# Batched transposed matmul on one core: b loaded with four consecutive rows in each partition, the column order restored in the PSUM copy, and stores three batches behind

## The chip, the cores and the metric

The kernel runs on one core of a Trainium2 chip. The metric is the device time of the whole program in microseconds, as a median of several executions. The span of the profile is some 1.6 to 2 us shorter than that time, because it runs from the first instruction to the last. All comparisons below are of runs that were classed as fast, except the two single-look probes, whose state is unknown; of those I use only durations within one trace.

Engine names in the profile: PE is the matmul engine, PEld its weight loads, DVE the vector engine, ACT the scalar engine, SPq the queue of the engine that issues all DMAs. SBUF is the on-chip memory that the DMAs of this kernel load and store, PSUM the one that PE writes its results to; the tiles that this kernel keeps in either have 128 rows (128x512 in the profile), called partitions.

## The reference

```
batch, m, k, n = 16, 512, 512, 512
a: (batch, k, m) float32,  b: (batch, n, k) float32
out = matmul(a transposed to (batch, m, k), b transposed to (batch, k, n))   # float32
```

Each batch reads 1 MiB of a and 1 MiB of b and writes 1 MiB. The total is 50.3 MB of traffic.

## The kernel before

b has n in its rows, and the matmuls of this kernel take k in the partitions. So PE transposes b in 128x128 blocks into PSUM, a copy on DVE casts the result to bf16 in SBUF, and 16 matmuls per batch use it. ACT casts a. The output is copied from PSUM by ACT and DVE in turns, and it is stored six batches later.

```python
a_v = a.rearrange("b (ki ko) m -> b ki ko m", ko=KO)      # 4 consecutive rows per partition: 8 KB
b_v = b.rearrange("b (no ni) k -> b ni no k", ni=P)       # 4 rows, 128 apart: 4 x 2 KB
# a_pool 3, b_pool 3, ac_pool 4, bt_pool 3, o_pool 8 buffers; PSUM: 4 for the transposes, 4 for the output
LAG = 6
for i in range(B):
    # load b, load a, four ACT casts of a (a_bf)                                        [cut]
    for rk in range(KO):
        bt_ps = psum_t.tile([P, N], f32)
        for no in range(NO):
            nc.tensor.transpose(bt_ps[:, no * P:(no + 1) * P], b_sr[:, no, rk, :], identity)
        nc.vector.tensor_copy(bt_sb[:, rk, :], bt_ps)             # fp32 PSUM -> bf16 SBUF
    for rm in range(MO):
        o_ps = psum_o.tile([P, N], f32)
        for rk in range(KO):
            nc.tensor.matmul(o_ps, a_br[:, rk, rm, :], bt_sb[:, rk, :], ...)
        # copy o_ps to o_sb on ACT (rm even) or DVE (rm odd)                              [cut]
    if i >= LAG: emit_out_dma(i - LAG)
```

Of the kernel before, what the change touches and what calls it, by code (L numbers as in the profile page):

```python
# [1 line left out]

# [5 lines left out]


@with_exitstack
def kernel(
    ctx: ExitStack,
    tc: tile.TileContext,
    a: bass.AP,
    b: bass.AP,
    out: bass.AP,
):
    nc = tc.nc
    P = 128  # L20
    B, K, M = a.shape
    _, N, _ = b.shape
    KO = K // P
    MO = M // P
    NO = N // P

    f32 = mybir.dt.float32
    cdt = mybir.dt.bfloat16

    a_v = a.rearrange("b (ki ko) m -> b ki ko m", ko=KO)  # L30
    b_v = b.rearrange("b (no ni) k -> b ni no k", ni=P)
    out_v = out.rearrange("b (mi mo) n -> b mi mo n", mo=MO)

    const = ctx.enter_context(tc.tile_pool(name="const", bufs=1))
    identity = const.tile([P, P], f32)
    make_identity(nc, identity)

    a_pool = ctx.enter_context(tc.tile_pool(name="a_pool", bufs=3))
    b_pool = ctx.enter_context(tc.tile_pool(name="b_pool", bufs=3))
    ac_pool = ctx.enter_context(tc.tile_pool(name="ac_pool", bufs=4))  # L40
    bt_pool = ctx.enter_context(tc.tile_pool(name="bt_pool", bufs=3))
    o_pool = ctx.enter_context(tc.tile_pool(name="o_pool", bufs=8))
    psum_t = ctx.enter_context(tc.tile_pool(name="psum_t", bufs=4, space=bass.MemoryType.PSUM))
    psum_o = ctx.enter_context(tc.tile_pool(name="psum_o", bufs=4, space=bass.MemoryType.PSUM))

    LAG = 6
    o_tiles = {}

    def emit_out_dma(j):
        nc.sync.dma_start(out_v[j], o_tiles.pop(j))  # L50

    for i in range(B):
        b_sb = b_pool.tile([P, NO, K], f32)
        nc.sync.dma_start(b_sb, b_v[i])
        a_sb = a_pool.tile([P, KO, M], f32)
        nc.sync.dma_start(a_sb, a_v[i])  # L56

        a_bf = ac_pool.tile([P, KO, M], cdt)
        for rk in range(KO):
            nc.scalar.copy(a_bf[:, rk, :], a_sb[:, rk, :])  # L60
        a_br = a_bf.rearrange("p rk (pm rm) -> p rk rm pm", rm=MO)

        b_sr = b_sb.rearrange("p no (pk rk) -> p no rk pk", rk=KO)
        bt_sb = bt_pool.tile([P, KO, N], cdt)
        for rk in range(KO):
            bt_ps = psum_t.tile([P, N], f32)
            for no in range(NO):
                nc.tensor.transpose(  # L68
                    bt_ps[:, no * P:(no + 1) * P],
                    b_sr[:, no, rk, :],  # L70
                    identity,
                )
            nc.vector.tensor_copy(bt_sb[:, rk, :], bt_ps)  # L73

        o_sb = o_pool.tile([P, MO, N], f32)
        o_tiles[i] = o_sb
# [3 lines that stand above are left out]
                nc.tensor.matmul(  # L80
                    o_ps,
                    a_br[:, rk, rm, :],
                    bt_sb[:, rk, :],
                    start=(rk == 0),
                    stop=(rk == KO - 1),
                )
            if rm % 2 == 0:
                nc.scalar.copy(o_sb[:, rm, :], o_ps)  # L88
            else:
                nc.vector.tensor_copy(o_sb[:, rm, :], o_ps)  # L90

        if i >= LAG:
            emit_out_dma(i - LAG)

    for j in range(B - LAG, B):
        emit_out_dma(j)


# [1 line left out]
_INS = ['a', 'b']  # L100
_OUTS = [((16, 512, 512), 'float32')]


# [23 lines left out]
```

## Time and profile before

| | before |
|---|---|
| time | 129.39 us (129.38 to 129.58) |
| span of the profile | 127.8 us |
| DMA, mean rate over the span | 394 GB/s |
| PE / DVE / ACT busy | 72% / 48% / 43% |
| DVE cast of bt_sb | 683 ns |

These lines of the page show the busy share by engine, the busy tenths in 40 equal slices of the span for PE, DVE and DMA, what the DMA moved in each slice, and the packets.

```profile
PE 92.5 (72%) x504; PEld 60.6 (47%) x512; DVE 61.5 (48%) x96; ACT 54.8 (43%) x97; POOL 0.7 (1%) x6
...
PE   0099999999999995768767796877779777670000
...
DVE  0053668586774865463544727355472635640000
...
DMA  3999999999999999999999999999999999999980
GB/s 90 402 370 422 406 399 420 382 409 398 404 417 415 417 419 394 416 410 429 420 410 423 406 436 405 416 426 413 427 402 431 412 424 418 426 428 428 426 346 36
DMA packets 13063, 50.42 MB, mean 394 GB/s; under 512 B 768, under 2 KB 768, under 8 KB 8960
```

The DMA row is the one without gaps: the kernel is bound by DMA. PE is full only from the 3rd slice to the 15th (to 48 us), where it works through batches whose loads came faster than it could follow.

The group of lines for the cast of b gives its duration (busy us, mean ns of one, then idle time before it and who ended it):

```profile
L73 DVE CAST bt_sb<-bt_ps 128x512 bf16<-128x512 f32 x64 | 40.0, 683 | 14.7 <-PE bt_ps L68 14.7
```

### The profile page before, as it was taken

The numbers are of one execution on the slowest core, as the hardware profiler recorded it, in microseconds if no ns is written. First come the engines' busy times: TensorE is split into PE (matmuls) and PEld (weight loads), VectorE is DVE, ScalarE is ACT, GpSimd is POOL, SyncE is SP. The second block draws the span as 40 slices with busy tenths as digits, with TensorE's granted clock in tenths as the row PEclk, the third lists the DMA queues.
The fourth block names the chain that finished last, engine by engine and source line by source line (L and its number), as shares of the span: only waits on it lengthen the run. The fifth ranks groups of instructions, "written<-read, shape, count | busy, mean of one in ns | idle before, by whom it ended". The sixth has DMA issues, their size and how long they took to land.

```text
span 127.8 us, 1405 instructions
## 1 busy us (share of the span) xinstructions
PE 92.5 (72%) x504; PEld 60.6 (47%) x512; DVE 61.5 (48%) x96; ACT 54.8 (43%) x97; POOL 0.7 (1%) x6
## 2 busy tenths in 40 slices
PE   0099999999999995768767796877779777670000
PEld 0094858678586763364634536353364634430000
DVE  0053668586774865463544727355472635640000
ACT  4026747646674635407163460816337072540000
POOL 2000000000000000000000000000000000000000
PEclk9999999999999999999999999999999999998555
DMA  3999999999999999999999999999999999999980
GB/s 90 402 370 422 406 399 420 382 409 398 404 417 415 417 419 394 416 410 429 420 410 423 406 436 405 416 426 413 427 402 431 412 424 418 426 428 428 426 346 36
DMA packets 13063, 50.42 MB, mean 394 GB/s; under 512 B 768, under 2 KB 768, under 8 KB 8960
## 3 DMA queue, kind: packets, MB, share of 16 engines
q1 hardware_dynamic: 13056, 50.33, 97.5%
q8 instruction: 4, 0.07, 0.2%
q14 instruction: 3, 0.02, 0.0%
HBM read 33.55 MB, written 16.78 MB: 394 GB/s over the span
## 4 chain that ended last, share of the span: by engine, by line
DMA 50%; PE 34%; SPq 3%; ACT 1%; issue 1%; DVE 1%; ACTq 0%
DMA a_sb<-in_a_dram 32%; PE o_ps L80 22%; DMA out_dram<-o_sb 13%; PE bt_ps L68 12%; DMA b_sb<-in_b_dram 4%; SPq L56 3%; ACT a_bf L60 1%; DVE o_sb L90 1%; ACT o_sb L88 0%; ACTq L60 0%; SPq L50 0%
## 5 line engine op out<-in xcount | busy, mean ns | idle before, releaser
L80 PE MATMUL o_ps<-bt_sb,a_bf 128*128 128x512 bf16 x248 | 59.0, 385 | 9.1 <-ACT a_bf L60 8.7
L60 ACT CAST a_bf<-a_sb 128x512 bf16<-128x512 f32 x64 | 34.9, 615 | 39.6 <-DMA a_sb<-in_a_dram 39.5
L73 DVE CAST bt_sb<-bt_ps 128x512 bf16<-128x512 f32 x64 | 40.0, 683 | 14.7 <-PE bt_ps L68 14.7
L68 PE MATMUL bt_ps<-identity,b_sb 128*128 128x128 f32 x256 | 35.7, 295 | 12.8 <-DMA b_sb<-in_b_dram 12.8
L80 PEld LDWEIGHTS <-a_bf 128*128 128x128 bf16 x256 | 27.3, 115 | 35.8 <-ACT a_bf L60 17.7
L68 PEld LDWEIGHTS bt_ps<-identity,b_sb 128*128 128x128 f32 x256 | 33.9, 211 | 17.5 <-PE o_ps L80 8.5
L90 DVE COPY o_sb<-o_ps 128x512 f32<-128x512 f32 x32 | 22.1, 692 | 38.9 <-PE o_ps L80 21.9
L88 ACT COPY o_sb<-o_ps 128x512 f32<-128x512 f32 x32 | 18.8, 586 | 19.0 <-PE o_ps L80 18.9
L60 ACT ACT_TABLE_LOAD x1 | 1.3, 1283 | 0.7 <-PEq L111 0.7
masks.py:199 POOL TENSOR_SCALAR_AFFINE_SELECT identity<-identity 128x128 f32<-128x128 f32 x1 | 0.3, 292 | 0.1
masks.py:197 POOL MEMSET identity<- 128x128 f32 x1 | 0.2, 204 | 0.3 <-POOLq L111 0.3
L111 POOL MEMSET const-bfloat16-1.0<- 128x1 bf16 x1 | 0.1, 101 | 0.0
L111 POOL MEMSET const-uint8-127<- 128x1 uint8 x1 | 0.1, 101 | 0.0
L111 POOL MEMSET const-float32-0.0<- 128x1 f32 x1 | 0.1, 98 | 0.2 <-issue 0.2
L111 POOL MEMSET const-float32-1.0<- 128x1 f32 x1 | 0.1, 98 | 0.0
## 6 DMA issues: line engine op xcount, KB each, us to landing
b_sb<-in_b_dram SPq DMA_DIRECT2D x16, 1024.0 KB, 15.4
a_sb<-in_a_dram SPq DMA_DIRECT2D x16, 1024.0 KB, 17.3
out_dram<-o_sb SPq DMA_DIRECT2D x16, 1024.0 KB, 17.4
```

Of the source, the lines that this page charges most:

```text
L56: nc.sync.dma_start(a_sb, a_v[i])
L60: nc.scalar.copy(a_bf[:, rk, :], a_sb[:, rk, :])
L68: nc.tensor.transpose(bt_ps[:, no * P:(no + 1) * P], b_sr[:, no, rk, :], identity,)
L73: nc.vector.tensor_copy(bt_sb[:, rk, :], bt_ps)
L80: nc.tensor.matmul(o_ps, a_br[:, rk, rm, :], bt_sb[:, rk, :], start=(rk == 0), stop=(rk == KO - 1),)
L88: nc.scalar.copy(o_sb[:, rm, :], o_ps)
L90: nc.vector.tensor_copy(o_sb[:, rm, :], o_ps)
L111: nc = _bacc.Bacc("TRN2", target_bir_lowering=False, num_devices=1)
```

## The change

The intent is to make the loads of b cheaper. With rows 4p to 4p+3 in partition p, each partition gets one contiguous piece of 8 KB instead of four of 2 KB. The transposed blocks then hold every fourth column, so the copy from PSUM puts the columns back in order by writing bf16 with a step of four elements, 8 bytes. Along with that the stores come three batches behind, and the buffers are redistributed.

```diff
-    b_v = b.rearrange("b (no ni) k -> b ni no k", ni=P)
+    b_v = b.rearrange("b (ni no) k -> b ni no k", no=NO)
...  a_pool 3 -> 5, b_pool 3 -> 5, ac_pool 4 -> 3, o_pool 8 -> 6 buffers
-    LAG = 6
+    LAG = 3
...
+        bt_w = bt_sb.rearrange("p rk (ni no) -> p rk no ni", no=NO)
         for rk in range(KO):
-            bt_ps = psum_t.tile([P, N], f32)
+            bt_ps = psum_t.tile([P, NO, P], f32)
...          transposes: same blocks
-            nc.vector.tensor_copy(bt_sb[:, rk, :], bt_ps)
+            nc.vector.tensor_copy(bt_w[:, rk, :, :], bt_ps)
```

More of the change, by code (lines that the diff above doesn't have):

```diff
@@ L36 @@
     make_identity(nc, identity)
-    a_pool = ctx.enter_context(tc.tile_pool(name="a_pool", bufs=3))
-    b_pool = ctx.enter_context(tc.tile_pool(name="b_pool", bufs=3))
-    ac_pool = ctx.enter_context(tc.tile_pool(name="ac_pool", bufs=4))
+    a_pool = ctx.enter_context(tc.tile_pool(name="a_pool", bufs=5))
+    b_pool = ctx.enter_context(tc.tile_pool(name="b_pool", bufs=5))
+    ac_pool = ctx.enter_context(tc.tile_pool(name="ac_pool", bufs=3))
     bt_pool = ctx.enter_context(tc.tile_pool(name="bt_pool", bufs=3))
-    o_pool = ctx.enter_context(tc.tile_pool(name="o_pool", bufs=8))
+    o_pool = ctx.enter_context(tc.tile_pool(name="o_pool", bufs=6))
     psum_t = ctx.enter_context(tc.tile_pool(name="psum_t", bufs=4, space=bass.MemoryType.PSUM))
     psum_o = ctx.enter_context(tc.tile_pool(name="psum_o", bufs=4, space=bass.MemoryType.PSUM))
-    LAG = 6
+    LAG = 3
     o_tiles = {}
-    def emit_out_dma(j):
-        nc.sync.dma_start(out_v[j], o_tiles.pop(j))
     for i in range(B):
@@ L64 @@
         bt_sb = bt_pool.tile([P, KO, N], cdt)
+        bt_w = bt_sb.rearrange("p rk (ni no) -> p rk no ni", no=NO)
         for rk in range(KO):
-            bt_ps = psum_t.tile([P, N], f32)
+            bt_ps = psum_t.tile([P, NO, P], f32)
             for no in range(NO):
-                nc.tensor.transpose(
-                    bt_ps[:, no * P:(no + 1) * P],
-                    b_sr[:, no, rk, :],
-                    identity,
-                )
-            nc.vector.tensor_copy(bt_sb[:, rk, :], bt_ps)
+                nc.tensor.transpose(bt_ps[:, no, :], b_sr[:, no, rk, :], identity)
+            nc.vector.tensor_copy(bt_w[:, rk, :, :], bt_ps)
         o_sb = o_pool.tile([P, MO, N], f32)
@@ L92 @@
         if i >= LAG:
-            emit_out_dma(i - LAG)
+            nc.sync.dma_start(out_v[i - LAG], o_tiles.pop(i - LAG))
     for j in range(B - LAG, B):
-        emit_out_dma(j)
+        nc.sync.dma_start(out_v[j], o_tiles.pop(j))
 _INS = ['a', 'b']
```

## The prediction

> **What bounds the kernel.** The 16 DMA engines. The page's slices show DMA at 9 (90% or more) in 37 of 40, 97.5% of the span on one queue; PE is busy 72%, DVE 48%, ACT 43%. The chain that ended last is half DMA; its PE half is the first 44 us, where the table of windows shows the DMA just as busy (400 to 410 GB/s). Packets run from 1.9 us to about 1.2 us before the span's end (127.8 us; the measured time is 1.6 us more). So only cheaper DMA traffic, or a gap in it, moves the time; the bytes (50.3 MB) stay.
>
> **The traffic.** b arrives as 8192 packets of 2 KB, a and out as 4096 of 8 KB. With four consecutive rows per partition b becomes 2048 packets of 8 KB. In the trace's packet records a 2 KB packet takes 84 ns (mean 86), an 8 KB one 309 (mean 313): 4 x 86 - 313 = 32 ns saved, x 2048 / 16 engines = 4.1 us. But successive packets overlap, small ones more: fitting the length of busy windows to the packets in them gives 82.5 and 310 ns, 2.5 us. Window rates agree: 403 GB/s where only a and b load, 417 with all three, 429 for stores alone, so b runs at 390 to 398 against about 425, 2.6 to 3.3 us over 16 MiB. [...] this trace shows several per cent at 2 KB, small but on the bounding resource. I take 3 us, all on the critical path.
>
> **The PSUM copy** now writes bf16 with a step of 8 bytes (683 ns now). [...] DVE has slack: 6 x 0.69 = 4.1 us of work per batch of about 7.2 us. PE and ACT: unchanged.
>
> **Lag 3, five load buffers.** Stores mix with loads earlier. No starvation: a store waits for the compute of three batches ago while 6 MB or more (over 14 us) are queued. The tail: after the last a lands, four stores remain (now seven), 2.45 us each on an engine, so the last store must be queued within 7.4 us of that landing. Landing to last copy took 5.1 us (110.0 to 115.1), plus 0.4 before it and 1.1 from issue to first packet: 6.7 us. It just fits on the slowest engine; faster engines may idle without setting the end. So lag costs 0 to 0.7 us and gains nothing.
>
> **Prediction.** 129.4 - 3.0 = 126.4 us, 8 in 10 within 125.3 to 127.6. Faster by over 2%: 0.60; within 2%: 0.38; slower: 0.02.
>
> **What would show it right or wrong.** DMA view: about 6,900 packets in all, mean rate from 394 to about 404 GB/s, DMA still 9 nearly throughout; b's packets at about 312 ns; the cast of bt_sb below 0.75 us; the last store issued before those ahead of it end, with perhaps a short dip of DMA just before the end.
>
> **What would make it wrong.** 8 KB loads mixed with stores running slower than now; a slow strided copy (over 1.2 us), which would delay the last batch and open a gap in the tail; small packets costing only what the fit of the later half says (80.4 and 309.8 ns, about 1.5 us)[...].

The sum of the forecast is 129.4 - 3.0 = 126.4 us, where the 3.0 us come from the packet records and window rates. The PSUM copy had no term in it. It was put at 0.75 us at most, and as that was below what DVE had to spare, it entered the sum with nothing. That bound was not worked out from a trace.

## More of the kernel before

How long does compute take for a batch when nothing holds it up? The timeline of the kernel before, in that first part, shows it (columns: start us, duration us, engine, line, operation, operands, count).

```profile
19.52 2.07 PE L68 MATMUL bt_ps<-identity,b_sb 128*128 128x128 f32 x16
...
20.33 2.48 DVE L73 CAST bt_sb<-bt_ps 128x512 bf16<-128x512 f32 x4
...
21.43 3.62 PE L80 MATMUL o_ps<-bt_sb,a_bf 128*128 128x512 bf16 x16
...
24.89 2.08 PE L68 MATMUL bt_ps<-identity,b_sb 128*128 128x128 f32 x16
```

From one group of transposes to the next is 24.89 - 19.52 = 5.37 us.

## The result

The changed kernel takes 134.68 us (134.66 to 134.71, 4 runs) against 129.40 us for the kernel before on the same chip. The ratio is 1.041 with a 95% interval of 1.040 to 1.043: slower by 4%. Here and below a ratio is the mean time of one kernel's fast runs over that of the other's fast runs of the same rounds, so it is not quite the ratio of the medians quoted beside it. The output is correct.

The same lines of the page, after:

```profile
PE 97.1 (73%) x504; PEld 62.4 (47%) x512; DVE 96.9 (73%) x96; ACT 53.3 (40%) x97; POOL 0.7 (1%) x6
...
PE   0297959786886959687786959788695959788620
...
DVE  0096787969597786959696896959687795959720
...
DMA  3999999999999999999999999999999999925124
GB/s 118 424 419 427 434 427 318 429 392 422 419 429 432 429 424 429 419 424 429 429 424 427 422 424 429 427 419 429 424 424 432 427 429 424 404 106 237 79 118 200
DMA packets 6919, 50.42 MB, mean 379 GB/s; under 512 B 768, under 2 KB 768, under 8 KB 768
```

Two things stand out. In mid-run (slices 11 to 34) the DMA moves 426 GB/s on average, where the kernel before moved 416, so the larger packets do what they should. But from the 36th slice on the DMA row falls from 9 to 2, 5, 1, 2, 4: for the last 16 us the DMA engines mostly wait. Busy time of DVE went from 61.5 to 96.9 us, and one group accounts for it:

```profile
L71 DVE CAST bt_sb<-bt_ps 128x512 bf16<-128x512 f32 x64 | 76.0, 1327 | 6.8 <-PE bt_ps L70 6.8
```

The copy with a step takes 1327 ns instead of 683. The timeline shows what that does to one batch:

```profile
21.35 2.08 PE L70 MATMUL bt_ps<-identity,b_sb 128*128 128x128 f32 x16
...
22.16 4.76 DVE L71 CAST bt_sb<-bt_ps 128x512 bf16<-128x512 f32 x4
...
23.54 0.59 PE L78 MATMUL o_ps<-bt_sb,a_bf 128*128 128x512 bf16 x2
...
26.97 1.89 PE L78 MATMUL o_ps<-bt_sb,a_bf 128*128 128x512 bf16 x8 [0.34 <-DVE bt_sb L71]
...
28.70 2.09 PE L70 MATMUL bt_ps<-identity,b_sb 128*128 128x128 f32 x16
```

PE transposes; the four copies take 4.76 us instead of 2.48; the last matmuls wait for the fourth copy ("<-DVE bt_sb L71"); and in the order in which PE runs them here the transposes of the next batch come only after those matmuls. The period is now 28.70 - 21.35 = 7.35 us, and 7.55 us from the fourth batch to the last. That is 2.0 to 2.2 us more than before, the 2.28 us that the four copies grew by, nearly.

What does the DMA need per batch? Three transfers at 2.45 us each on an engine (the spacing of completions in the trace's packet records), so 7.4 us. The two periods are nearly equal, and that is why the loss is easily misread. While a batch is in flight the DMA has work, and its row is full. But compute, at 7.5 us per batch from the first batch on, needs 5.7 us (first b landed) + 16 x 7.5 = 126 us before the last output can be stored; it ends at 127.7 us, and the last store lands at 131.7 us, near the end of the span at 132.9 us. In the kernel before, compute could run at 5.4 us per batch while the first loads, without stores between them, were coming in at 403 GB/s (16 to 28 us), an estimated 5.2 us for the two of a batch (2.1 MB); it followed the loads closely and was done at 115.1 us, 5.1 us after the last a was seen to land.

### The profile page after: what moved, and what is told of

Its sections match the earlier page's. It is cut to its first block, busy times and chain, and to the rows that moved or that the text cites. A ratio compares the mean times of both kernels' runs of the same rounds, so it can differ in the third digit from the quotient of the medians.

```text
span 132.9 us, 1387 instructions
## 1 busy us (share of the span) xinstructions
PE 97.1 (73%) x504; PEld 62.4 (47%) x512; DVE 96.9 (73%) x96; ACT 53.3 (40%) x97; POOL 0.7 (1%) x6
## 5 line engine op out<-in xcount | busy, mean ns | idle before, releaser
L78 PE MATMUL o_ps<-bt_sb,a_bf 128*128 128x512 bf16 x248 | 64.8, 378 | 24.2 <-DVE bt_sb L71 22.3
L71 DVE CAST bt_sb<-bt_ps 128x512 bf16<-128x512 f32 x64 | 76.0, 1327 | 6.8 <-PE bt_ps L70 6.8
L78 PEld LDWEIGHTS <-a_bf 128*128 128x128 bf16 x256 | 29.2, 114 | 56.7 <-issue 38.1
L70 PE MATMUL bt_ps<-identity,b_sb 128*128 128x128 f32 x256 | 34.9, 292 | 5.7 <-DMA b_sb<-in_b_dram 5.7
L70 PEld LDWEIGHTS bt_ps<-identity,b_sb 128*128 128x128 f32 x256 | 34.6, 210 | 7.5 <-issue 5.6
```

The lines of the kernel that those rows point to most:

```text
L70: nc.tensor.transpose(bt_ps[:, no, :], b_sr[:, no, rk, :], identity)
L71: nc.vector.tensor_copy(bt_w[:, rk, :, :], bt_ps)
```

## Experiments

The theory (A): the copy with the step of 8 bytes takes twice as long, it stands in a serial chain from PE to DVE and back to PE, and that chain became the limit. The rivals (B): three batches of lag starve the DMA queue, or the 8 KB rows load worse. The wait table of the issuing queue makes the first rival look strong, so it had to be tested. In the changed kernel (columns: us in total, times, longest us):

```profile
SPq L91 <- DVE o_sb L88: 80.4, 13, 10.0
SPq L94 <- DVE o_sb L88: 21.5, 3, 7.2
```

The queue waits 80 us for the compute of three batches ago, which looks like starvation.

### 1. The copy without its step (wrong column order on purpose)

```diff
-            nc.vector.tensor_copy(bt_w[:, rk, :, :], bt_ps)
+            nc.vector.tensor_copy(bt_sb[:, rk, :].rearrange("p (no ni) -> p no ni", no=NO), bt_ps)
```

> The changed kernel, with the PSUM copy writing without a step (so the columns of the output come in the wrong order: wrong on purpose). Theory A (the copy with a step takes twice as long and makes the chain PE, DVE, PE longer than the DMA's time per batch): casts back at 0.68 us, 126 to 127 us, ratio to before 0.975 to 0.985, DMA without the hole at the end. Theory B (three batches of lag starve the DMA queue, or 8 KB rows load more slowly): still 132 us or more.

Measured: 126.58 us (126.39 to 126.72), ratio 0.978 (0.976 to 0.980); casts 683 ns. Everything else of the change is in this kernel, lag included. So the step of the copy is the whole of the loss, and it hides a gain of 2.2%.

### 2. The step alone, in the kernel before (wrong column order on purpose)

```diff
+        bt_w = bt_sb.rearrange("p rk (ni no) -> p rk no ni", no=NO)
-            nc.vector.tensor_copy(bt_sb[:, rk, :], bt_ps)
+            nc.vector.tensor_copy(bt_w[:, rk, :, :], bt_ps.rearrange("p (no ni) -> p no ni", no=NO))
```

> The kernel before, with only the copy's step of four elements added (lag 6, three load buffers, 2 KB rows; columns in the wrong order on purpose). Theory A: 16 batches at 7.5 us after the first b has landed at 6.4 us, plus 5 us of last store: 131 to 135 us, ratio 1.02 to 1.045. Theory B: 129 to 130 us, as before.

Measured: 134.94 us, ratio 1.042 (1.040 to 1.044). The step alone costs as much as the whole change. Once the chain is the limit, cheaper loads are worth little: this kernel with 2 KB rows and the changed one with 8 KB rows are both at 1.04. The kernel that differs from this one by the 8 KB rows alone is that of experiment 3, at 134.24 us. The 0.7 us between them is what the first b gains: the transposes start at 6.33 us here and at 5.69 us there, and the last output copy ends 0.66 us later here.

### 3. The changed kernel with the old lag and buffers

```diff
-    LAG = 3          a 5, b 5, cast a 3, out 6 buffers
+    LAG = 6          a 3, b 3, cast a 4, out 8 buffers
```

> The changed kernel with the old lag of 6 and the old numbers of buffers (a and b 3, cast a 4, out 8). Theory A: the chain of compute is unchanged, 133 to 136 us, ratio 1.03 to 1.05. Theory B: under 128 us, because the DMA queue no longer waits for the compute of three batches ago.

Measured: 134.24 us, ratio 1.037 (1.035 to 1.039). The lag is not the cause: the last output copy ends at 127.7 us in both traces. The 0.4 us by which the time is below that of the changed kernel come after that copy, and what they are was not looked into. The queue's wait did not vanish but moved to another line:

```profile
SPq L53 <- PE bt_ps L70: 75.5, 13, 6.5
SPq L94 <- DVE o_sb L88: 25.2, 4, 7.2
```

Now the loads of b wait 75.5 us for a buffer, which the transposes release. Whatever paces the batches, the issuing queue waits for it somewhere; such a wait tells that the queue is ahead, not that it is starved. In experiment 1 the same wait on L91 was still 40.3 us, at a DMA that was never idle in mid-run.

### 4. The changed kernel's lag and buffers alone, in the kernel before

```diff
-    LAG = 6          a 3, b 3, cast a 4, out 8 buffers
+    LAG = 3          a 5, b 5, cast a 3, out 6 buffers
```

> The kernel before with only the lag of 3 and the new numbers of buffers (2 KB rows, copy without a step). The prediction said that the lag gains nothing and costs 0 to 0.7 us: 129.2 to 130.2 us, ratio 0.998 to 1.006. A rival: the earlier mixing of stores and loads gains by itself, under 128.5.

Measured: 129.53 us against 129.35, ratio 1.0005 (0.999 to 1.002). In this kernel the lag neither gains nor costs.

### 5. A probe of the step

In one kernel, the four copies of each batch write bf16 with steps of 1, 2, 4 and 8 elements, and the matmuls read them back with the same step. Its output is wrong, which doesn't matter for the time. To make room, a and b have 3 buffers here and bt_sb 2.

```diff
+  bt_v = [bt_sb[:, r, :N << r].rearrange("p (n s) -> p s n", s=1 << r)[:, 0, :] for r in range(KO)]
+  if rk == 0:   nc.vector.tensor_copy(bt_v[0], ...)     # L72, step 2 bytes
+  elif rk == 1: nc.vector.tensor_copy(bt_v[1], ...)     # L74, 4 bytes
+  elif rk == 2: nc.vector.tensor_copy(bt_v[2], ...)     # L76, 8 bytes
+  else:         nc.vector.tensor_copy(bt_v[3], ...)     # L78, 16 bytes
+  # matmuls that read bt_v[0..3]: L87, L89, L91, L93
```

> A probe, wrong on purpose: within each batch the four copies from PSUM write bf16 with steps of 1, 2, 4 and 8 elements (2, 4, 8, 16 bytes), each on its own line, and the matmuls read them back with the same step, each on its own line. A1 [...]: 0.68 us at step 1, 1.33 at 2, 4 and 8. A2 (the distance counts): step 2 under 1.0, step 8 well over 1.33. The matmuls that read with a step: 0.38 us for all if reading with a step is free, over 0.5 if not.

Its groups of lines (mean ns is the second number after the bar):

```profile
L93 PE MATMUL o_ps<-bt_sb,a_bf 128*128 128x512 bf16 x64 | 66.2, 1077 | 16.3 <-DVE bt_sb L78 16.3
...
L78 DVE CAST bt_sb<-bt_ps 128x512 bf16<-128x512 f32 x16 | 39.6, 2477 | 0.0
L91 PE MATMUL o_ps<-bt_sb,a_bf 128*128 128x512 bf16 x64 | 37.2, 624 | 1.2 <-DVE bt_sb L76 1.2
...
L89 PE MATMUL o_ps<-bt_sb,a_bf 128*128 128x512 bf16 x64 | 26.4, 450 | 0.1
L87 PE MATMUL o_ps<-bt_sb,a_bf 128*128 128x512 bf16 x56 | 22.8, 447 | 0.4
...
L76 DVE CAST bt_sb<-bt_ps 128x512 bf16<-128x512 f32 x16 | 20.7, 1295 | 0.7
...
L72 DVE CAST bt_sb<-bt_ps 128x512 bf16<-128x512 f32 x16 | 11.0, 688 | 8.5 <-PE bt_ps L70 8.5
L74 DVE CAST bt_sb<-bt_ps 128x512 bf16<-128x512 f32 x16 | 11.8, 739 | 1.3 <-PE bt_ps L70 1.3
```

The DVE write takes 688, 739, 1295 and 2477 ns at steps of 2, 4, 8 and 16 bytes. So hypothesis A1 of the expectation (any step loses) is refuted and A2 (the distance counts) holds: a step of two elements is almost free, and beyond that each doubling of the step about doubles the time. Matmuls that read bt_sb with a step take 447, 450, 624 and 1077 ns by the same lines. These means blur the effect: PE's granted clock was only 0.81 of full speed in this probe, and the profile models where a matmul ends. Two matmuls of the same line in a row start 216 ns apart without a step (at the full clock), 229, 433 and 881 ns apart with steps of 4, 8 and 16 bytes, so reading doubles at the same distances as writing. With 16 matmuls per batch, the step of 8 bytes would have added an estimated 16 x (433 - 216) = 3.5 us per batch to PE, more than the copies lost, so reading bt_sb with a step in the matmul would have been no way out either.

### 6. Two rows in each partition: 4 KB packets and a step of 4 bytes

```diff
-    b_v = b.rearrange("b (ni no) k -> b ni no k", no=NO)
+    b_v = b.rearrange("b (nb ni n2) k -> b ni nb n2 k", ni=P, n2=2)
-        bt_w = bt_sb.rearrange("p rk (ni no) -> p rk no ni", no=NO)
+        bt_w = bt_sb.rearrange("p rk (nb ni n2) -> p rk nb n2 ni", ni=P, n2=2)
```

> The changed kernel with two consecutive rows of b in each partition instead of four: packets of 4 KB, and the copy writes bf16 with a step of 2 elements (4 bytes), which the step probe showed nearly free (0.74 us, 0.63 us apart). Correct result. If the step of the write is the whole cause (A): casts at 0.74 us, 5.5 to 5.7 us per batch where compute is alone, so DMA-bound: 126.6 to 127.8 us, ratio 0.977 to 0.987 (two thirds of the gain of 8 KB packets). If an interleaved write as such were the cause: 131 us or more.

Measured: 126.78 us, ratio 0.981 (0.979 to 0.983), casts 727 ns, correct. An interleaved write is not slow as such; its distance is what counts. The trace's packet records give a median of 159 ns for a 4 KB packet, so 318 ns for 8 KB, against 4 x 84 = 336 ns in packets of 2 KB and 309 ns in one of 8 KB.

### 7. Four ways to restore the order, in one kernel

```diff
+  rk == 1: the transposes write PSUM with a step of 16 bytes (L71), the copy has no step (L77)
+  rk == 0: nc.vector.tensor_copy(bt_sb[:, rk, :] as (ni no), bt_ps.rearrange("p no ni -> p ni no"))   # L75
+  rk == 2: nc.scalar.copy(bt_w[:, rk, :, :], bt_ps)                                                 # L79
+  rk == 3: nc.vector.tensor_copy(bt_w[:, rk, :, :], bt_ps)             # L81, as in the changed kernel
```

> A probe with a correct result: the changed kernel, with the reorder done in four ways, one for each rk of a batch: DVE reads PSUM with a step of 512 bytes and writes without a step; PE writes the transpose into PSUM with a step of 16 bytes and DVE copies without one; ACT copies with the step of 8 bytes; DVE as in the changed kernel (control, 1.33 us). If only writing to SBUF with a step is slow: the first two casts 0.68 us, the transposes as before (about 0.29 us, 0.13 apart). If stepping through PSUM costs as well: over 1.0 us for the first. ACT: 0.6 us if it has no such cost, over 1.0 if it does.

```profile
L73 PE MATMUL bt_ps<-identity,b_sb 128*128 128x128 f32 x192 | 30.0, 294 | 7.0 <-DMA b_sb<-in_b_dram 6.4
...
L81 DVE CAST bt_sb<-bt_ps 128x512 bf16<-128x512 f32 x16 | 20.8, 1298 | 1.9 <-PE bt_ps L73 0.9
L79 ACT CAST bt_sb<-bt_ps 128x512 bf16<-128x512 f32 x16 | 20.7, 1294 | 26.0 <-PE bt_ps L73 26.0
...
L75 DVE CAST bt_sb<-bt_ps 128x512 bf16<-128x512 f32 x16 | 11.0, 687 | 8.8 <-PE bt_ps L73 8.8
L77 DVE CAST bt_sb<-bt_ps 128x512 bf16<-128x512 f32 x16 | 10.9, 682 | 0.2 <-PE bt_ps L71 0.2
L71 PE MATMUL bt_ps<-identity,b_sb 128*128 128x128 f32 x64 | 10.8, 292 | 0.0
```

The result is correct. Reading PSUM with a step of 512 bytes costs nothing (687 ns), and neither does writing the transposes into PSUM with a step of 16 bytes (292 ns against 294, transposes starting 121 ns apart in both, and a copy of 682 ns); no run wrote the 128x512 outputs of the bf16 matmuls with a step. Writing SBUF with the step of 8 bytes costs ACT the same as DVE, 1294 ns, where ACT's copies of the fp32 outputs from PSUM, which write without a step, took 586 ns. The cost belongs to the SBUF side.

### 8. The slow copies kept, but out of the chain

If the loss comes from the chain, then putting the transposes and copies of batch i+1 ahead of the matmuls of batch i should remove it, with the copies as slow as ever. The order on PE and DVE was pinned in the program, so that the scheduler could not restore the old one.

```diff
+    for i in range(B + 1):
+        # loads, casts, transposes and stepped copies of batch i   (if i < B)
+        # matmuls and output copies of batch i - 1                 (if i > 0)
```

> The changed kernel, slow copies and all, but the transposes and copies of batch i+1 are put ahead of the matmuls of batch i on PE and DVE, so the slow copies no longer stand in a serial chain with PE. Correct result. If the loss comes from the serial chain (2.1 transposes to 4.75 copies to 1.9 matmuls, 7.5 us per batch): DVE's own work of 4.6 + 1.4 = 6.0 us per batch is below the DMA's 7.4, so 126.5 to 128.5 us, ratio 0.977 to 0.993, casts still 1.33 us. If the DVE's throughput alone were the limit, or the slow writes hurt the DMA: still over 131 us.

Measured: 128.71 us (128.04 to 128.98), ratio 0.993 (0.991 to 0.996), casts 1348 ns, correct. The slow copies alone thus did not decide the time: 6 of the 8 us between the changed kernel and experiment 1 return by a new order. It came out just above the range I expected. The rest is paid after the last load, as the timeline shows:

```profile
112.15 2.17 PE L70 MATMUL bt_ps<-identity,b_sb 128*128 128x128 f32 x16 [1.74 <-DMA b_sb<-in_b_dram]
112.91 4.80 DVE L71 CAST bt_sb<-bt_ps 128x512 bf16<-128x512 f32 x4 [1.45 <-PE bt_ps L70]
...
114.17 7.07 PE L83 MATMUL o_ps<-bt_sb,a_bf 128*128 128x512 bf16 x31
...
121.27 0.69 DVE L93 COPY o_sb<-o_ps 128x512 f32<-128x512 f32 x1 [0.98 <-PE o_ps L83]
```

The matmuls of the last two batches now both follow the last transposes, and the last output copy ends at 122.0 us, against 119.1 us in experiment 1.

### 9. The order restored on the reading side

```diff
-        bt_w = bt_sb.rearrange("p rk (ni no) -> p rk no ni", no=NO)
+        bt_w = bt_sb.rearrange("p rk (ni no) -> p rk ni no", no=NO)
-            nc.vector.tensor_copy(bt_w[:, rk, :, :], bt_ps)
+            nc.vector.tensor_copy(bt_w[:, rk, :, :], bt_ps.rearrange("p no ni -> p ni no"))
```

> The changed kernel with the reorder moved to the other side of the copy: it reads PSUM with a step of 512 bytes and writes SBUF without one. Correct result. The probe of reorders gave 0.69 us for this form, so by theory A: casts at 0.68 to 0.70 us, 5.4 us per batch where compute is alone, DMA-bound, 126.2 to 126.9 us, ratio 0.975 to 0.980, as with the wrong-ordered copy without a step. If something else in the change cost time: over 128 us.

Measured: 126.40 us (126.28 to 126.76), ratio 0.977 (0.975 to 0.979), correct. It beats both kernels. Its page:

```profile
DMA  3999999999999999999999999999999999999973
GB/s 97 423 428 428 426 420 365 384 415 407 423 431 428 431 426 423 418 426 428 434 420 423 420 426 431 420 418 431 428 426 423 426 426 431 431 420 423 415 331 142
DMA packets 6919, 50.42 MB, mean 404 GB/s; under 512 B 768, under 2 KB 768, under 8 KB 768
...
L71 DVE CAST bt_sb<-bt_ps 128x512 bf16<-128x512 f32 x64 | 40.0, 684 | 14.8 <-PE bt_ps L70 14.8
```

The DMA row is full again to the 38th slice. The same data go to the same places as in the changed kernel; only the side of the copy that takes the step differs.

### 10. The same with the old lag and buffers

```diff
-    LAG = 3          a 5, b 5, cast a 3, out 6 buffers
+    LAG = 6          a 3, b 3, cast a 4, out 8 buffers
```

> The same with the old lag of 6 and the old numbers of buffers, so the kernel before with only the 8 KB rows and a reorder that costs nothing. If the shorter lag costs nothing (its last store is in the queue before the slowest engine runs dry): 126.0 to 126.9 us, within 0.5% of the run with lag 3. If the lag costs its predicted 0.7 us or more at the end: 125.9 or less.

Measured: 126.60 us, ratio 0.978 (0.977 to 0.979), beside 0.977 with lag 3. So the 8 KB rows with a free reorder bring the 2.2 to 2.3% alone, and the lag does nothing here either.

## Why the prediction was wrong

The step that failed is the one on the PSUM copy, "the cast of bt_sb below 0.75 us". It measured 1.33 us. The bound did not come from a measurement: the only copy of bt_sb in the trace of the kernel before writes without a step (683 ns), and no run with a stepped write had been made. Experiment 5 supplied what was missing: writes of 512 columns of bf16 with steps of 2, 4, 8 and 16 bytes took 688, 739, 1295 and 2477 ns. A step of 4 bytes would have kept the bound, the step of 8 bytes that the change uses does not. Such a probe before the prediction would have shown it.

The second failure follows from the first. "DVE has slack: 6 x 0.69 = 4.1 us of work per batch of about 7.2 us" counted the engine's work against the batch, and even with slow copies that sum is only about 6 us (4 x 1.15 apart, + 2 x 0.69); DVE is busy 73% in the slow kernel. But the copies stand between the transposes and the matmuls of the same batch, and PE does not start the next transposes before those matmuls. In such a chain the time that counts is the time along it, 7.55 us per batch, not the largest share. The prediction named a slow copy among what could make it wrong, but expected it to "delay the last batch"; it delayed every batch. Experiments 1, 2 and 8 show this: the copy alone costs what the change costs, without its step the loss is gone, and out of the chain most of it is gone though the copy is as slow as ever.

The other steps held:

- The kernel before is DMA-bound, and 8 KB packets save about 3 us. Experiment 10 isolates this: 129.41 to 126.60, 2.8 us. The prediction of 126.4 us for the whole is what experiments 1 and 9 gave once the copy was free (126.58 and 126.40). That it fits so closely is partly luck: the prediction's own estimates of the saving ran from 2.5 to 4.1 us, and it took 3.
- The packet count (about 6,900) was right, and so was the duration of 8 KB packets (mean 314 ns in the changed kernel, predicted 312). The mean rate of 404 GB/s was not reached by the changed kernel (379), but by experiment 9, where the copy was free.
- The lag of three gains nothing and costs 0 to 0.7 us: 0.05% in experiment 4, within 0.1% in experiments 9 and 10, and the changed kernel lies 0.4 us above experiment 3, inside that range.
- The tail "just fits on the slowest engine": in the trace of experiment 1 the 16 completions of the last store come at 122.6 to 123.3 us, those of the store before at 118.4 to 120.9. Taken in order (the packet records that were kept do not name the engine), some engines pause for up to 1.8 us before the last store, and the slowest passes to it without a pause (120.88 and 123.33 us, 2.45 apart).

What stays open is why the step costs what it costs. The runs show the dependence on the distance for writes of bf16 by DVE and at one distance by ACT, and for matmul reads; they do not show the mechanism.

## What to carry to other kernels

When a layout change must be paid for with a reorder somewhere, measure what the step costs on each side of the copy: here writing it to SBUF doubled the copy (683 to 1327 ns), and reading it from PSUM was free (684 ns), so the same change is either 4% slower or 2% faster. Before calling an engine's spare time slack, follow one unit of work through the timeline and add up the chain that the order of the instructions makes of it. A long wait of the DMA-issuing queue only says that something else sets the pace; it does not show that the queue's lag is at fault (here 80.4 us with a lag of 3 and 75.5 us, on another line, with a lag of 6).
